# A decoder layer on one core: the last expert pair by rows with its scatter summed in PSUM, the overflow loop moved to behind pair 11, and the last normalization of both tiles interleaved

## The chip, the cores and the metric

The kernel runs on one core of a Trainium2 chip. The metric is device time in microseconds (us) of one launch. Engines are named as the profile names them: PE is the matrix engine (PEld its weight loads), DVE the vector engine, ACT the scalar engine, POOL the GpSimd engine and SP the engine whose queue issues nearly all weight transfers. A DMA is one such transfer, and it "lands" when its semaphore says that the data are there.

## What is computed

One layer for 256 tokens of width 1024: an attention and retention block, a cross attention over 256 memory tokens, and a mixture of 32 experts, each followed by a layer normalization. The change touches the experts and the last normalization alone.

```python
def moe(x, router_w, router_b, w_gate, b_gate, w_up, b_up, w_down, b_down):
    logits = xf @ router_w + router_b
    top_val, top_idx = lax.top_k(logits, 4)
    top_w = jax.nn.softmax(top_val, axis=-1)
    ...
    def step(y, blk):
        e, tok, wt = blk
        xb = xf[tok]
        gate = jnp.minimum(xb @ w_gate[e] + b_gate[e], 7.0)
        up = jnp.clip(xb @ w_up[e] + b_up[e], -7.0, 7.0)
        hmid = gate * jax.nn.sigmoid(1.702 * gate) * (up + 1.0)
        out = hmid @ w_down[e] + b_down[e]
        return y.at[tok].add(out * wt[:, None])
...
f = moe(x, ...)
x = layer_norm(DEEPNORM_ALPHA * x + f, ln3_g, ln3_b)
```

All arithmetic is float32. The three weights of an expert hold 4 MB each, so the 32 experts bring 403 MB through the DMA queues.

## The kernel before

The first part of the layer (attention, retention, cross attention, router) takes about the first 265 us and is not touched.

The experts are worked in 16 pairs, pr = 0 to 15. A pair has 64 token slots for each of its two experts, so 128 rows in all. For each pair: `masks` (L934, DVE) builds the one-hot matrix `oh` of tokens and slots; `gather` (L951 on PE, L955 on ACT) picks the tokens' columns into `xg`; `ff` (L991 bias, L983 products) multiplies by `w_gate`, then by `w_up`; `gate` (L1007 to L1009) and `swiglu` (L1015, L1016) apply the activation on DVE and ACT; `h_t` (L1025, L1026) transposes the result; `down` (L983) multiplies by `w_down` and `scaled` (L976, ACT) weighs the rows; `back` (L964, L966) transposes `oh`; and `scatter` (L1046 on PE, L1047 on DVE) adds the rows onto the two token tiles of the sum `y`. The scatter of pair pr is done inside `ff` of `w_gate` of pair pr+1, after its first quarter, and the gather of pair pr+1 stands between `w_up` and `w_down` of pair pr.

The order on each engine is written out by hand, in program order. Weights stream through SBUF in tiles of 2 MB ("doubles": half of one expert's weight): four tiles for each weight of a pair, twelve for a pair. `stream_get` takes two tiles at a time, and `pump_doubles` issues the next loads in the list whenever enough doubles are free; about ten of them are in use or in flight. All these loads wait in one queue, that of SP (L1083), and SP issues a load when the tile's former readers are done and the load eight places earlier has landed.

The last pair stands apart (L1249 onward). Its `w_up` and the first half of its `w_down` come in 512-column parts and the second half in 256-column parts, in 16 and 18 smaller loads. The products are made column by column (`cols_mm`, L1257): after each part of `down` follow `scaled`, `scatter` and the normalization's statistics (L613) for those columns. Then the hand-written order is closed and `extra` (L1177) runs: a loop over a number read at run time, for experts that got more than 64 tokens. With these inputs it runs zero times, but its branches and the meeting of all engines ahead of it remain. Behind it `Norm.finish` handles tile 0, then tile 1: L617 mean and variance, L368 and L369 (POOL) the reciprocal root, L632 centring, L638 scaling, and L1290 the four output transfers.

Of the kernel before, what the change touches and what calls it, by code (L numbers as in the profile page):

```python
# [28 lines left out]
AHEAD = 3  # L29
SLOTS = (1, 10, 18, 13, 20, 7, 19, 17, 16, 14, 5, 3, 0, 2, 21, 9, 8, 11, 6, 12, 15, 4)  # L30
# [44 lines left out]
def _body(tc, nc, ctx, I, out, dbg):  # L75
# [7 lines left out]
    manual.enter_context(tc.manual_schedule())  # L83

# [505 lines left out]
    class Norm:  # L590
# [3 lines left out]
        def __init__(self, o, g, b, z=None):  # L594
            self.o, self.g, self.b, self.z = o, g, b, z
            self.bs = sm.tile([P, 2, 4, 6], F32, name="bs", tag="bs")
            self.mv = sm.tile([P, 2, 4], F32, name="mv", tag="mv")
# [12 lines left out]
        def stats(self, t, cs):  # L610

            for q in range(cs.start // 256, cs.stop // 256):
                nc.vector.bn_stats(out=self.bs[:, t, q, :], in_=self.o[t][:, 256 * q:256 * q + 256])  # L613

        def rstd(self, t, n=2):
            mv = self.mv[:, t, :]
            nc.vector.bn_aggr(out=mv[:, 0:2], in_=self.bs[:, t, 0:n])  # L617
            rsqrt_eps(mv[:, 2:3], mv[:, 1:2], 1)
# [10 lines left out]
        def center(self, t):  # L629
            for c in range(2):  # L630
                y = self.o[t][:, half[c]]
                nc.vector.scalar_tensor_tensor(out=y, in0=y, scalar=self.mv[:, t, 0:1], in1=self.g[:, half[c]],  # L632
# [9 lines left out]

        def finish(self, t, each=None):
            self.rstd(t, 4)
            self.center(t)
            self.scale(t, each)
# [347 lines left out]
    def ff(xg, selt, j, get, mid=None):  # L994
        ps = biased(selt, j)
        for kk in range(4):
# [4 lines left out]
            if kk == 0 and mid:  # L1001
                mid()
# [39 lines left out]
    def scatter(o, ohT, cs=half, after=None):  # L1042
        for c in cs:
            for t in range(2):
                py = tr_tile()[:, 0:c.stop - c.start]
                nc.tensor.matmul(py, ohT[:, tok[t]], o[:, c], start=True, stop=True)  # L1046
                nc.vector.tensor_tensor(out=y[t][:, c], in0=y[t][:, c], in1=py, op=ALU.add)  # L1047
                if after:
                    after(t, c)
# [6 lines left out]

    for pr in range(1, NPAIR):
        for n in ("w_gate", "w_up", "w_down")[:3 if pr < NPAIR - 1 else 1]:
            for a in range(2):
                for e in range(2):  # L1060
                    loads.append(([4, D], [(0, lambda t: t, fours(I[n][0, 2 * pr + e])[:, a])]))

    def col_parts(n, c0, cn, k0, *ks):

        for a, b in zip(ks, ks[1:]):
            for e in range(2):
                yield e, lambda t, a=a, b=b: t[:, k0 + a:k0 + b, :], \
                    fours(I[n][0, NE - 2 + e])[:, a // 4, a % 4:a % 4 + b - a, c0:c0 + cn]


    for c in range(2):
        loads.append(([KC, 512], [*col_parts("w_up", 512 * c, 512, 0, 0, 4, 8)]))
    loads.append(([KC, 512], [*col_parts("w_down", 0, 512, 0, 0, 4, 6, 8)]))
    loads.append(([2 * KC, 256], [*col_parts("w_down", 512, 256, 0, 0, 4, 8),
                                  *col_parts("w_down", 768, 256, KC, 0, 4, 6, 8)]))

    def load_double():

        shape, parts = loads.pop(0)
        ts = [tile8(shape, weight=True, n=2) for _ in range(1 + max(e for e, _, _ in parts))]  # L1080
        got.extend(ts)
        for e, dst, src in parts:
# [92 lines left out]
    def extra():  # L1175

        with tc.For_i(0, n_extra, 1) as i:  # L1177
# [32 lines left out]
            scatter(down(h_t(u, as_t(ta)), getter("w_down"), ohT, tb), ohT, after=n3.stats)  # L1210
# [16 lines left out]

    prev = None
    oh = static_masks(0)
    selt = static_pick(0)  # L1230
    xg = gather(oh)
    for pr in range(NPAIR - 1):
# [4 lines left out]
        ps = ff(xg, selt, 0, stream_get, (lambda: scatter(*prev)) if pr else None)  # L1237
# [5 lines left out]
        oh = static_masks(pr + 1)  # L1243
# [84 lines left out]
```

## Time and profile before

| | us |
|---|---|
| median of 3 runs (lowest, highest) | 1182.46 (1181.59, 1185.07) |
| time of the profiled execution | 1185.23 |
| its span, first to last instruction | 1183.3 |
| PE busy | 1124.9 (95%) |
| DVE, ACT, POOL busy | 323.8, 233.9, 28.5 |
| bytes moved by DMA | 447.66 MB, 378 GB/s over the span |

The table's busy times are sums over the whole span. How far an engine is the bound differs by stretch, and the rows further down are read by stretch: a row of a timeline is a run of like instructions on one engine, with its start, its length, and in brackets the idle time ahead of it and what ended it.

### The profile page before, as it was taken

The numbers are of one execution on the slowest core, as the hardware profiler recorded it, in microseconds if no ns is written. First come the engines' busy times: TensorE is split into PE (matmuls) and PEld (weight loads), VectorE is DVE, ScalarE is ACT, GpSimd is POOL, SyncE is SP. The second block draws the span as 40 slices with busy tenths as digits, with TensorE's granted clock in tenths as the row PEclk, the third lists the DMA queues.
The fourth block names the chain that finished last, engine by engine and source line by source line (L and its number), as shares of the span: only waits on it lengthen the run. The fifth ranks groups of instructions, "written<-read, shape, count | busy, mean of one in ns | idle before, by whom it ended". The sixth has DMA issues, their size and how long they took to land. (4 is left out here: it accounts for less than half of the span.)

```text
span 1183.3 us, 12818 instructions
## 1 busy us (share of the span) xinstructions
PE 1124.9 (95%) x5473; PEld 558.4 (47%) x5473; DVE 323.8 (27%) x461; ACT 233.9 (20%) x433; POOL 28.5 (2%) x37
## 2 busy tenths in 40 slices
PE   8999999999999999999999998989899989999985
PEld 6788899864333434343343434343334343433332
DVE  5666866662121110112110101010101010102114
ACT  5543455431010101010111011010011010120100
POOL 0102300100000000000000000000000000000000
PEclk9999999999989999999999999999999999989998
DMA  9937538589999999999999999999999999999994
GB/s 333 388 125 280 183 133 320 185 349 415 417 397 417 431 425 429 427 428 428 428 428 427 429 426 428 428 427 430 425 429 427 426 430 425 430 427 428 414 372 141
DMA packets 60928, 447.66 MB, mean 378 GB/s; under 512 B 5186, under 2 KB 10050, under 8 KB 35524
## 3 DMA queue, kind: packets, MB, share of 16 engines
q1 hardware_dynamic: 60484, 446.15, 91.7%
q8 instruction: 45, 0.74, 0.3%
q10 hardware_dynamic: 384, 0.66, 0.2%
q14 instruction: 15, 0.12, 0.0%
HBM read 445.73 MB, written 1.05 MB: 378 GB/s over the span
## 5 line engine op out<-in xcount | busy, mean ns | idle before, releaser
L983 PE MATMUL mm<-t,t 128*64 128x512 f32 x2944 | 670.0, 602 | 21.6 <-DMA t<-in_w_up_dram 18.3
L983 PEld LDWEIGHTS mm<-t,t 128*64 128x64 f32 x2944 | 217.6, 138 | 445.9 <-issue 406.7
L1047 DVE TENSOR_TENSOR t<-t,tr 128x512 f32<-128x512 f32 (+1 forms) x66 | 44.2, 670 | 376.0 <-PE tr L1046 376.0
L256 PE MATMUL mm<-t,t 128*128 128x512 f32 (+1 forms) x368 | 129.4, 352 | 1.1 <-ACT t L142 1.1
L257 PE MATMUL mm<-t,t 128*128 128x512 f32 (+1 forms) x368 | 127.0, 345 | 1.0 <-DVE t L143 1.0
L258 PE MATMUL mm<-t,t 128*128 128x512 f32 (+1 forms) x368 | 126.7, 344 | 0.0
L955 ACT ACTIVATE t<-tr,gb 128x128 f32<-128x128 f32 x128 | 48.2, 456 | 259.4 <-PE tr L951 240.4
L143 DVE TENSOR_TENSOR t<-t,t 128x1024 fp32r<-128x1024 f32 (+2 forms) x74 | 86.3, 1181 | 31.2 <-ACT t L142 30.7
L1015 DVE TENSOR_SCALAR mm<-mm 128x512 f32<-128x512 f32 x32 | 22.4, 699 | 216.0 <-PE mm L983 202.7
L142 ACT CAST t<-t 128x1024 fp32r<-128x1024 f32 (+1 forms) x76 | 73.8, 999 | 37.7 <-DVE t L143 15.0
L1008 ACT ACTIVATE t<-mm 128x1024 f32<-128x1024 f32 x16 | 16.4, 1024 | 301.7 <-DVE mm L1007 301.7
L256 PEld LDWEIGHTS mm<-t,t 128*128 128x128 f32 x368 | 69.8, 190 | 12.1 <-ACT t L142 2.7
L257 PEld LDWEIGHTS mm<-t,t 128*128 128x128 f32 x368 | 69.8, 190 | 9.5 <-DVE t L143 2.1
L258 PEld LDWEIGHTS mm<-t,t 128*128 128x128 f32 x368 | 69.8, 190 | 8.3
L1046 PE MATMUL tr<-t,ohT 128*128 128x512 f32 (+1 forms) x132 | 62.6, 605 | 2.0 <-ACT t L976 1.4
L951 PEld LDWEIGHTS tr<-oh,t 128*128 128x128 f32 x512 | 58.4, 192 | 12.6 <-issue 12.2
L951 PE MATMUL tr<-oh,t 128*128 128x128 f32 x512 | 61.4, 278 | 0.0
L1007 DVE TENSOR_SCALAR mm<-mm 128x1024 f32<-128x1024 f32 x16 | 19.7, 1233 | 152.1 <-PE mm L983 152.1
L976 ACT ACTIVATE t<-mm,ohT 128x1024 f32<-128x1024 f32 (+2 forms) x18 | 18.3, 1019 | 213.6 <-PE mm L983 196.5
L1046 PEld LDWEIGHTS tr<-t,ohT 128*128 128x128 f32 x132 | 21.1, 188 | 43.4 <-issue 19.8
L1025 PE MATMUL tr<-ident,t 128*128 128x128 f32 x128 | 23.6, 307 | 17.1 <-ACT t L955 15.5
L1257 PE MATMUL mm<-t,t 128*64 128x512 f32 (+1 forms) x160 | 28.8, 511 | 1.6 <-DVE t L1016 1.6
(166 smaller groups left out, 471.8 us busy)
## 6 DMA issues: line engine op xcount, KB each, us to landing
t<-in_w_gate_dram SPq DMA_DIRECT2D x60, 2048.0 KB, 35.0
t<-in_w_up_dram SPq DMA_DIRECT2D x56, 2048.0 KB, 34.0
t<-in_w_down_dram SPq DMA_DIRECT2D x56, 2048.0 KB, 31.7
t<-in_w_up_dram SPq DMA_DIRECT2D x16, 1024.0 KB, 10.5
t<-in_w_in_dram SPq DMA_DIRECT2D x12, 1024.0 KB, 14.2
t<-in_w_down_dram SPq DMA_DIRECT2D x10, 1024.0 KB, 11.4
t<-in_w_gate_dram SPq DMA_DIRECT2D x8, 1024.0 KB, 7.0
t<-in_w_down_dram SPq DMA_DIRECT2D x10, 512.0 KB, 10.9
```

Source lines behind the costliest of these rows:

```text
L142: h(out=hi, in_=src)
L143: l(out=lo, in0=src, in1=hi.bitcast(F32))
L256: nc.tensor.matmul(ps, lh, rh, start=start, stop=False)
L257: nc.tensor.matmul(ps, lh, rl, start=False, stop=False)
L258: nc.tensor.matmul(ps, ll, rh, start=False, stop=stop)
L951: nc.tensor.matmul(px[:, c, :], zn[t][:, chunk(4 * j + c)], oh[:, t, :], start=(c == 0 and t == 0), stop=(c == 3 and t == 1))
L955: nc.scalar.activation(out=xg[:, k, :], in_=px[:, c, :], func=AF.Identity, scale=gb[:, 0, k:k + 1], bias=gb[:, 1, k:k + 1])
L983: nc.tensor.matmul(ps[r, half[c]], lhs[:, 2 * kk + k, r], w(e, k), start=(first and k == 0), stop=(last and k == 1))
L1025: nc.tensor.transpose(ph[:, c, :], u[:, cols(4 * j + c)], ident)
L1046: nc.tensor.matmul(py, ohT[:, tok[t]], o[:, c], start=True, stop=True)
L1047: nc.vector.tensor_tensor(out=y[t][:, c], in0=y[t][:, c], in1=py, op=ALU.add)
L1257: nc.tensor.matmul(ps[r, :], lhs[:, k0 + k, r], w[e][:, j0 + k, :], start=(k0 + k == 0 and lhs is not xg), stop=(k0 + k == KC - 1))
```

## The change

Three things are done.

The overflow loop `extra` moves from the end to behind pair 11 (`EXTRA = 11`). Pair 11 no longer has the gather of pair 12 between its products; it scatters its own rows at once, all engines meet at the loop, and `start_pair(12)` (masks, pick, gather) follows. While pair 11's `down` runs, `hold[0] = 3` keeps three doubles free for the loop's own tiles; the hold falls behind the loop. The load of the last normalization's two parameter rows (`load_rows`) comes behind the loop too, as its place in the program did not change.

The last pair's weights come by rows in nearly the same tiles as all other pairs', with the last four tiles of `w_up` and `w_down` cut into 1 MB and smaller loads. Its products run in the order of the other pairs. In the midst of its `w_up`, `y_sums` copies `y` into two PSUM tiles `ys` by a product with the identity, and the last scatter accumulates on them, so the four DVE additions of that scatter are gone. The swiglu, the first half of `h_t` and `down` now follow each other without overlap between column halves of `w_up`.

The last normalization reads `ys` in PSUM: statistics and centring of tile 0, statistics of tile 1, scaling of tile 0, centring and scaling of tile 1, with statistics over 512 columns at a time.

```diff
+EXTRA = 11
...
     def pump_doubles():
-        while loads and doubles() >= 1 + max(e for e, _, _ in loads[0][1]):
+        while loads and doubles() >= 1 + hold[0] + max(e for e, _, _ in loads[0]):
             load_double()
...
         ohT = static_back(oh, pr)
-        oh = static_masks(pr + 1)
+        if pr != EXTRA:
+            oh = static_masks(pr + 1)
         u = swiglu(ff(xg, selt, 1, stream_get, add_bias if pr == 1 else None), g)
-        xg, selt = gather(oh), static_pick(pr + 1)
+        if pr != EXTRA:
+            xg, selt = gather(oh), static_pick(pr + 1)
+        hold[0] = 3 if pr == EXTRA else 0
         prev = (down(h_t(u), stream_get, ohT, mid=spread_rows if pr == NPAIR - 3 else None), ohT)
...
+        if pr == EXTRA:
+            scatter(*prev)
+            prev = None
+            n_extra = nc.values_load(ni32[0:1, 0:1], min_val=0, max_val=3 * NPAIR)
+            manual.close()
+            extra()
+            manual.enter_context(tc.manual_schedule())
+            hold[0] = 0
+            oh, selt, xg = start_pair(pr + 1)
...
+    def y_sums():
+        ys.extend(mm_tile() for _ in range(2))
+        for t in range(2):
+            for c in half:
+                nc.tensor.matmul(ys[t][:, c], ident, y[t][:, c], start=True, stop=False)
+
+    u = swiglu(ff(xg, selt, 1, stream_get, {1: y_sums}), g)
+    hT = h_t(u, cs=(0,))
...
+                if kk == 3 and k == 1:
+                    scaled(o[:, half[c]], ps[:, half[c]], ohT)
+        done()
+        if kk == 0:
+            h_t(u, hT, (1,))
...
+    for t in range(2):
+        for c in range(2):
+            nc.tensor.matmul(ys[t][:, half[c]], ohT[:, tok[t]], o[:, half[c]], start=False, stop=True)
+            n3.stats(t, c)
+        n3.rstd(t)
+        if t == 0:
+            n3.center(0)
...
+    n3.scale(0, store)
+    n3.center(1)
+    n3.scale(1, store)
     manual.close()
-    extra()
-    for t in range(2):
-        n3.finish(t, each=lambda t, c: (nc.sync, nc.scalar)[c].dma_start(out=o_v[:, t, half[c]],
```

In the rows that follow, L1077 is the weight load (L1083 before), L1171 the loop, L1253 the reading of its count, L978 the products of a pair, L1042 the scatter, L946 the gather.

SP's queue around pair 12's `w_up`, before (tiles t_564 to t_569 are pair 12's `w_gate`, t_572 to t_577 its `w_up`, t_581 its `w_down`):

```order
L1083 DMA t_569_4574<-in_w_gate_dram 128x4096 [waits DMAHW3_49,PE_49]
L1083 DMA t_572_4639<-in_w_up_dram 128x4096 [waits DMAHW4_49,PE_49]
L1083 DMA t_573_4641<-in_w_up_dram 128x4096 [waits DMAHW5_49,PE_49]
L1083 DMA t_576_4659<-in_w_up_dram 128x4096 [waits DMAHW6_49,PE_49]
L1083 DMA t_577_4661<-in_w_up_dram 128x4096 [waits DMAHW7_49,PE_49]
L1217 DMA t_580_4681<-in_ln_g_dram 1x1024 [waits DMAHW0_49]
L1217 DMA t_580_4681<-in_ln_b_dram 1x1024 [waits DMAHW1_49]
L1083 DMA t_581_4687<-in_w_down_dram 128x4096 [waits DMAHW2_49,PE_49]
```

The same place of SP's queue in the changed kernel, up to the loop:

```order
L1077 DMA t_569_4572<-in_w_gate_dram 128x4096 [waits DMAHW3_49,PE_49]
L1077 DMA t_574_4624<-in_w_up_dram 128x4096 [waits DMAHW4_49,PE_49]
L1253 TENSOR_LOAD ni_2180 [waits DVE_49]
L1171 COMPARE_AND_BRANCH
L1171 UNCONDITIONAL_BRANCH [waits DMAHW0_49,DMAHW1_49,DMAHW2_49,DMAHW3_49,DMAHW4_49,DMAHW5_49,DMAHW6_49,DMAHW7_49]
```

And behind the loop:

```order
L1253 ISA x2
L1212 DMA t_583_4926<-in_ln_g_dram 1x1024
L1212 DMA t_583_4926<-in_ln_b_dram 1x1024
L1077 DMA t_584_4932<-in_w_up_dram 128x4096
L1077 DMA t_585_4934<-in_w_up_dram 128x4096
L1077 DMA t_586_4936<-in_w_up_dram 128x4096
L1077 DMA t_587_4938<-in_w_down_dram 128x4096
L1077 DMA t_588_4940<-in_w_down_dram 128x4096
L1077 DMA t_591_4958<-in_w_down_dram 128x4096 [waits PE_49]
```

One load of pair 12's `w_up` now stands ahead of the loop and three behind it, and at the branch SP waits for the semaphores of all eight DMA slots.

PE behind pair 11's `down` (t_560 and t_561 are the last two tiles of its `w_down`), in the changed kernel, up to the loop:

```order
L978 MATMUL mm<-t_561_4515,t_4594 64x512
L1042 MATMUL tr<-t_4642,ohT 128x512 [waits Activation_49]
L1042 MATMUL tr<-t_4642,ohT 128x512 [waits PE_49]
L1042 MATMUL tr<-t_4642,ohT 128x512 [waits DVE_49] x2
L1253 TENSOR_LOAD ni_2180 [waits DVE_49]
L1171 COMPARE_AND_BRANCH
L1171 UNCONDITIONAL_BRANCH [waits PE_49]
L1171 UNCONDITIONAL_BRANCH [waits barrier_Pool_Activation_PE_DVE_SP_release]
```

And behind it (t_564 and t_565 are pair 12's first `w_gate` tiles):

```order
L946 MATMUL tr<-oh,t_262_1997 128x128 [waits DVE_49]
L946 MATMUL tr<-oh,t_262_1997 128x128 x15
L986 MATMUL mm<-t_1996,selt 128x512 [waits DVE_49]
L986 MATMUL mm<-t_1996,selt 128x512
L978 MATMUL mm<-t_564_4550,t_4899 64x512 [waits Activation_49]
```

Before, the bias and the products of pair 12's `w_gate` stood straight behind that `down`; now the scatter, the meeting of the engines and the gather stand between them.

PE at the end of the changed kernel (t_5668 is `hT`, t_663 and t_664 the last tiles of `w_down`, t_5676 is `o`):

```order
L1281 MATMUL mm<-t_663_5583,t_5668 64x512 [waits DMAHW2_49,Activation_49]
L1281 MATMUL mm<-t_664_5584,t_5668 64x512 [waits DMAHW3_49]
L1292 MATMUL mm<-t_5676,ohT 128x512
L1292 MATMUL mm<-t_5676,ohT 128x512 [waits DVE_49,Activation_49]
L1292 MATMUL mm<-t_5676,ohT 128x512
L1292 MATMUL mm<-t_5676,ohT 128x512 [waits DVE_49]
```

All four scatter products now stand behind the whole of `down`, where two of them stood between its column parts.

## Rows read from the trace of the kernel before

**Rows 1.** Page, span in 40 equal slices: what the DMA queues moved.

```profile
GB/s 333 388 125 280 183 133 320 185 349 415 417 397 417 431 425 429 427 428 428 428 428 427 429 426 428 428 427 430 425 429 427 426 430 425 430 427 428 414 372 141
```

**Rows 2.** DMA view: issues, count, KB each, median us from issue to landing.

```profile
t<-in_w_gate_dram SPq DMA_DIRECT2D x60, 2048.0 KB, 35.0
...
out_dram<-t SPq DMA_DIRECT2D x2, 256.0 KB, 2.1
```

**Rows 3.** Timeline of SP's queue: start, length, operation; pair 12's w_up loads.

```profile
911.16 14.77 SPq L1083 DMA_DIRECT2D t<-in_w_up_dram  x4
```

**Rows 4.** Timeline of PE, pairs 11 to 14: start, length, operation, idle before.

```profile
904.89 7.08 PE L983 MATMUL mm<-t,t 128*64 128x512 f32 x30 [2.20 <-DMA t<-in_w_up_dram]
911.90 3.84 PE L951 MATMUL tr<-oh,t 128*128 128x128 f32 x32
...
918.02 13.95 PE L983 MATMUL mm<-t,t 128*64 128x512 f32 x64
931.90 0.73 PE L991 MATMUL mm<-t,selt 64*128 64x512 f32 x2
...
937.85 3.89 PE L1046 MATMUL tr<-t,ohT 128*128 128x512 f32 x8
...
963.63 7.08 PE L983 MATMUL mm<-t,t 128*64 128x512 f32 x30 [2.20 <-DMA t<-in_w_up_dram]
...
990.64 0.73 PE L991 MATMUL mm<-t,selt 64*128 64x512 f32 x2
...
1022.73 8.78 PE L983 MATMUL mm<-t,t 128*64 128x512 f32 x30 [2.56 <-DMA t<-in_w_up_dram]
...
1044.57 4.43 PE L1225 MATMUL tr<-t,ones_f 1*128 1x512 f32 x8
1048.93 9.78 PE L983 MATMUL mm<-t,t 128*64 128x512 f32 x32
1058.64 0.73 PE L991 MATMUL mm<-t,selt 64*128 64x512 f32 x2
```

**Rows 5.** Stretches: us, busy of PE to POOL (count), granted clock, DMA share, GB/s.

```profile
1020.00:1030.00 10.00, 7.44 (x28) 2.33 (x28) 0.00 (x0) 0.00 (x0) 0.00 (x0) 0.83 1.02 434
...
1130.00:1140.00 10.00, 9.38 (x46) 3.31 (x42) 3.00 (x3) 1.48 (x4) 0.00 (x0) 1.00 1.05 386
```

**Rows 6.** Timeline of PE, pair 14's down and the last pair.

```profile
1098.53 13.95 PE L983 MATMUL mm<-t,t 128*64 128x512 f32 x64
...
1112.41 0.73 PE L991 MATMUL mm<-t,selt 64*128 64x512 f32 x2
...
1132.29 7.09 PE L1257 MATMUL mm<-t,t 128*64 128x512 f32 x32
...
1159.05 1.98 PE L1046 MATMUL tr<-t,ohT 128*128 128x512 f32 x4 [0.85 <-ACT t L976]
...
1166.28 3.67 PE L1257 MATMUL mm<-t,t 128*64 128x256 f32 x32
```

**Rows 7.** Timeline of DVE, pair 14's mask and swiglu, and the end.

```profile
1080.82 0.42 DVE L934 TENSOR_TENSOR oh<-posm,iota 128x256 f32<-128x256 f32 x1
1092.55 0.70 DVE L1015 TENSOR_SCALAR mm<-mm 128x512 f32<-128x512 f32 x1 [11.31 <-PE mm L983]
...
1094.75 0.69 DVE L1016 SCALAR_TENSOR_TENSOR t<-mm,t 128x512 f32<-128x512 f32 x1
...
1160.94 0.75 DVE L613 BATCH_NORM_STATS2 bs<-t 128x6 f32<-128x256 f32 x2
...
1174.23 0.26 DVE L617 BATCH_NORM_AGGREGATE mv<-bs 128x2 f32<-128x24 f32 x1 [1.30 <-issue]
...
1174.85 1.41 DVE L632 SCALAR_TENSOR_TENSOR t<-t,mv,t 128x512 f32<-128x512 f32 x2
...
1178.88 1.41 DVE L638 SCALAR_TENSOR_TENSOR t<-t,mv,t 128x512 f32<-128x512 f32 x2
```

**Rows 8.** The loop's line on PE: count, ns min/median/max, first and last start.

```profile
L1177 PEldq COMPARE_BRANCH  x3: 97/196/3782, 1170.6 to 1176.6; - x3
```

More of the change, by code (lines that the diff above doesn't have):

```diff
@@ L608, in take, with stats, rstd @@
             nc.vector.bn_stats(out=self.bs[:, t, c, :], in_=y)
[L610 to L615, printed above, removed]
+        def stats(self, t, c):
+            nc.vector.bn_stats(out=self.bs[:, t, c, :], in_=self.src[t][:, half[c]])
+        def rstd(self, t):
             mv = self.mv[:, t, :]
-            nc.vector.bn_aggr(out=mv[:, 0:2], in_=self.bs[:, t, 0:n])
+            nc.vector.bn_aggr(out=mv[:, 0:2], in_=self.bs[:, t, 0:2])
             rsqrt_eps(mv[:, 2:3], mv[:, 1:2], 1)
@@ L1000, in ff @@
             done()
-            if kk == 0 and mid:
-                mid()
+            if kk in mids:
+                mids[kk]()
         return ps
@@ L1040, in down, with scatter @@
         return o
-    def scatter(o, ohT, cs=half, after=None):
-        for c in cs:
+    def scatter(o, ohT):
+        for c in half:
             for t in range(2):
-                py = tr_tile()[:, 0:c.stop - c.start]
+                py = tr_tile()
                 nc.tensor.matmul(py, ohT[:, tok[t]], o[:, c], start=True, stop=True)
                 nc.vector.tensor_tensor(out=y[t][:, c], in0=y[t][:, c], in1=py, op=ALU.add)
-                if after:
-                    after(t, c)
     wpos = [NPRE]
@@ L1209, in extra @@
             u = swiglu(ff(xg, selt, 1, getter("w_up")), g)
-            scatter(down(h_t(u, as_t(ta)), getter("w_down"), ohT, tb), ohT, after=n3.stats)
+            scatter(down(h_t(u, as_t(ta)), getter("w_down"), ohT, tb), ohT)
+            free8(tab, *ws2)
     LN3 = {}
@@ L1226, in spread_rows, with start_pair @@
                 nc.scalar.copy(out=gb3[:, j, half[c]], in_=pt)
+    def start_pair(pr):
+        oh = static_masks(pr)
+        selt = static_pick(pr)
+        return oh, selt, gather(oh)
     prev = None
-    oh = static_masks(0)
-    selt = static_pick(0)
-    xg = gather(oh)
+    oh, selt, xg = start_pair(0)
     for pr in range(NPAIR - 1):
@@ L1236, in _body @@
             load_rows()
-        ps = ff(xg, selt, 0, stream_get, (lambda: scatter(*prev)) if pr else None)
+        ps = ff(xg, selt, 0, stream_get, (lambda: scatter(*prev)) if prev else None)
         if pr == 0:
@@ L1248, in _body @@
             tables()
-    n_extra = nc.values_load(ni32[0:1, 0:1], min_val=0, max_val=3 * NPAIR)
-    g = gate(ff(xg, selt, 0, stream_get, lambda: scatter(*prev)))
-    def cols_mm(ps, lhs, w, k0, j0):
-        for k in range(4):
-            for e in range(2):
-                r = slice(64 * e, 64 * e + 64)
-                nc.tensor.matmul(ps[r, :], lhs[:, k0 + k, r], w[e][:, j0 + k, :],
-                                 start=(k0 + k == 0 and lhs is not xg), stop=(k0 + k == KC - 1))
-    ohT = static_back(oh, NPAIR - 1)
@@ new lines, in _body @@
+    n3 = Norm(y, LN3["gb"][:, 0, :], LN3["gb"][:, 1, :], src=ys)
+    o_v = out.rearrange("(t p) d -> p t d", p=P)
+    for t in range(2):
+        for c in range(2):
+            nc.tensor.matmul(ys[t][:, half[c]], ohT[:, tok[t]], o[:, half[c]], start=False, stop=True)
[3 more added lines that the diff above has]
+            n3.center(0)
+    store = lambda t, c: (nc.sync, nc.scalar)[c].dma_start(out=o_v[:, t, half[c]], in_=y[t][:, half[c]])
+    n3.scale(0, store)
+    n3.center(1)
```

82 lines of the change are left out of this document (33 added, 49 removed).

## The prediction

> **What bounds the kernel now.** I read the stretches first, then PE's timeline, then SP's queue. Through the expert pairs the DMA queues move 425 to 430 GB/s without a break until the last slices [rows 1]. A weight tile of 2048 KB [rows 2] is 2.097 MB, so at 428 GB/s it takes 4.90 us, and twelve tiles, a pair, 58.8. PE's timeline bears it out: its waits for the fourth `w_up` tile of pair 11 and of pair 12 end at 904.89 and 963.63 [rows 4], 58.74 apart, which is 4.895 a tile. Where PE has no transfer to wait for it needs less for a pair: from pair 14's bias at 1058.64 [rows 4] to pair 15's at 1112.41 [rows 6] are 53.77 us, and no row of that stretch ends a wait for a DMA. So the stream is the bound until PE's last wait for it, which ends at 1022.73 [rows 4]; from there on PE is, because the work at 1044.57 and a low clock put it behind. What counts for the end is therefore when PE can run without waits, and how much work it then has.
>
> **The loop behind pair 11.** The meeting of the engines needs SP, and SP's branch waits for the semaphores of all eight DMA slots (the order of SP's queue). So PE cannot go on before everything in flight has landed. In flight at that point are the loads up to the first `w_up` tile of pair 12; that load's turn comes at 911.16 as before [rows 3], since nothing changes ahead of it. Behind the tile landed at 904.89 come four of pair 11's `w_down`, four of pair 12's `w_gate` and this one: 9 x 4.895 = 44.05, so the last lands at 948.94.
>
> PE itself is there long before. Its `down` of pair 11 must wait for its fourth tile (904.89 + 4 x 4.895 = 924.5), then half of 13.95 [rows 4] gives 931.5, the scaling about 1, the scatter 3.89 [rows 4]: 937. It idles 12 us. What I save in pair 11 (no gather between `w_up` and `down`) is swallowed by this wait and counts nothing.
>
> Restart. The branches and semaphores of the loop take DVE 1.30 from its last operation to its next at the end of the kernel before [rows 7]; then the mask 0.42 [rows 7], then the gather can start: 948.94 + 1.72 = 950.66. PE's own branch took up to 3.78 [rows 8]; it comes before the meeting and PE has 12 us for it, so I count 0 and keep 3.8 as the upper end. The gather takes 3.84 [rows 4], now with nothing beside it.
>
> The clock. After a wait of 2.56 us the granted clock of a stretch was 0.83 [rows 5], that is, some of it at 1.2 GHz in place of 2.4, and the half phase behind it took 8.78 where the one at 904.89 took 7.08: 1.7 lost. After the thin row products at 1044.57 a half took 9.78 in place of 7.09 [rows 4, 6]: 2.69 lost. Nothing shows 12 idle us; bounds are 0 and 3.8 (the whole gather at half rate), and I take 2.7, the costlier of the two rows, as the idle time is longer than either. A rule of the Trainium skill speaks against the change here: "TensorE: Matmul & The Clock Gate", Part 1: The HAM clock gate, says that the throttled clock is the default and that sustained activity releases it, so that work behind an idle engine begins at half rate. The two rows agree; by the rule the zero end falls away and the sum stays.
>
> So pair 12's `w_gate` phase starts at 950.66 + 3.84 + 2.7 = 957.2, against 931.90 before [rows 4]: 25.3 later.
>
> From there PE saves. First the scatter of pair 11, already done: 3.9. Second all waits: before, from 931.90 to 1112.41 three pairs took 180.51. Pair 12 took 58.74 (931.90 to 990.64), 4.97 over 53.77. Pair 13 took 68.00 (to 1058.64), 14.23 over; of that 4.36 is the parameter rows' spreading (1044.57 to 1048.93) and 2.69 the clock behind it, both of which stay, so 7.18 is waiting and its clock. Together 12.15. In the changed kernel PE is late enough that the tiles are there: at 957.2 all of pair 12's `w_gate` and one tile of `w_up` lie in SBUF. SP issues the next at about 948.94 + 1.3 + some 1.2 for its two small row loads; a transfer's landing costs some 2.1 beside its bytes (256 KB, [rows 2]), so the first lands near 958.5 and each next 4.9 later, three `w_up` tiles by 968.3, where PE wants the last near 980. That margin of 9 us and more holds in the later pairs, as PE takes 53.8 a pair plus the spreading's 7 and the stream 58.8.
>
> PE thus leaves pair 14 at 957.2 - 3.9 + 180.5 - 12.15 = 1121.7, against 1112.41: **9.3 us later**. The loads still to go are 43 tiles, the last landing near 958.5 + 42 x 4.9 = 1164; PE wants it at about 1173 (below).
>
> **The last pair.** Before, 1112.41 to the end of the last column part, 1166.28 + 3.67 = 1169.95 [rows 6]: 57.54. After, in order: bias, `w_gate` with scatter, `back` and bias 19.88 (1112.41 to 1132.29, [rows 6], unchanged); `w_up` 13.9 [rows 6]; the four identity products on `y`: two scatter products took 1.98 with their pipeline's end [rows 6], so 3.6 (3.4 to 4.0); swiglu with nothing beside it 2.9 (1092.55 to 1095.44, [rows 7]) and hand-overs, 3.2, in which the first transposes and their copy lie too; `down` 13.9 and the second transposes in it 0.6 (four of the gather's instructions at 3.84 / 32, and the hand-over). Sum 55.1, so **2.4 us less**. The rows in place of columns also bring the last 16 MB at 428 GB/s instead of 386 [rows 5], some 4 us of the stream, but PE waits for nothing there, so it counts nothing.
>
> The end. Before: 1169.95 to 1183.3, 13.35. After `down`: scaling of the second half overlaps the first product; four products of 0.9 in a row end at 3.5; statistics of tile 0 (0.75 for 512 columns, [rows 7]) end at 2.7, aggregation 0.4, then DVE is full: centring 1.4, statistics of tile 1 1.5, aggregation 0.4, scaling, centring, scaling 3 x 1.35 [rows 7], which ends at 10.4; from DVE's last row (1178.88 + 1.41 = 1180.29) to the span's end were 3.0. Sum 13.4, so **0**. What the loop cost there (1.3) and the four additions save is paid back by four scatter products in one row and by DVE's seven long operations behind them. Reading the sums from PSUM costs DVE nothing that shows: L1015 reads PSUM at 0.70 and L632 SBUF at half of 1.41 [rows 7].
>
> **Sum.** +9.3 - 2.4 + 0 = +6.9. The profiled execution took 1185.23, so 1192.1 by its own time. The median is 2.77 below it. Of that, 1.7 can be the low clock behind the wait at 1022.73, which the changed kernel does not have anyway, so I take off between 1.1 and 2.8: 1189.3 to 1191.0. I say **1190.0**.
>
> **Rivals.** *The meeting does not wait for the transfers.* Then the engines pass near 938, PE goes on and meets the stream as before, SP's five held loads go out at 939 against 914 to 944 before, so the stream never stops, and only the last pair's 2.4 are left: 1182.46 - 2.4 = 1180, within 0.3% of before (0.3%, 3.5 us, is about what a measurement of this kernel can tell from no change). For it: the loop runs zero times. Against it: SP's branch names all eight slots. It decides whether PE idles 1 or 13 us at the loop. 0.09.
>
> *PE's branch comes late.* If the code behind the jump is fetched only after the meeting, 3.78 is added [rows 8], and a longer stay at the low clock adds up to 1.1: 1194 to 1195. Against it: PE arrives 12 us early. 0.15.
>
> *The loss is smaller.* No time at the low clock (-2.7) and a little less in the last pair (statistics earlier, -1): 1186.3, at the edge of "slower". 0.10.
>
> *The stream becomes the bound again*, if its restart takes over 9 us more than I have it: each us beyond is a us at the end, 1191 and up. The rows show no such restart; 0.04.
>
> **How the numbers follow.** My forecast (1188 to 1192.5) has 0.62, the rivals 0.09, 0.15, 0.10 and 0.04. The range 1186 to 1194.5 takes in the clock's two ends, the identity products' 0.6 and the offset to the median, most of the late branch, and leaves out the first rival. Faster by over 0.3% (under 1178.9) would need the first rival with some us more from the last pair: 0.03. Within 0.3% (to 1186.0): the rest of the first rival and half of the third, 0.12. Slower: 0.85.
>
> **What would show it.** Right: PE idle some 13 us behind pair 11's scatter, near 937 to 951; GB/s down in one slice there and no wait of PE for a DMA behind it; pair 14's end near 1122; `down` of the last pair ending near 1177; DVE full from there to the last store. Wrong: an idle time near 1 us at the loop, or waits for `w_up` and `w_gate` tiles in pairs 13 and 14, which would mean that the stream and not PE sets the end.

## The result and the profile after

| | before | after |
|---|---|---|
| median (lowest, highest), 6 runs each | 1183.08 (1181.59, 1185.33) | 1194.97 (1190.11, 1196.92) |
| profiled execution, its span | 1185.23, 1183.3 | 1196.92, 1194.8 |
| mean granted clock of that execution | 0.986 | 0.976 |

The change costs 11.9 us: the ratio of after to before is 1.009, with an interval of 1.0063 to 1.0116. The forecast was 1190.0 and the range's top 1194.5, so direction and mechanism came as forecast, and the median lies 0.5 us above the range. The range was set on the first median of before, 1182.46; on that one the ratio of 1.009 makes 1193.1, inside it. The six runs of the changed kernel lie 6.8 us apart, more than those of before, and go with the mean granted clock: 0.987 and 0.988 in the runs of 1190.11 and 1190.17, 0.976 to 0.982 in the four from 1194.7 to 1196.92. The profiled execution is the slowest of the six.

The page's slices (each 29.9 us) show where the stream of weights stops. Slice 32 moves 322 GB/s, where the slices of before around it have 425 to 430 [rows 1], and its granted clock falls to 0.7.

```profile
PEclk9999999999989999999999999999999799999998
...
GB/s 333 385 108 282 183 138 315 194 350 417 416 398 416 427 428 427 427 430 427 427 428 428 428 427 427 428 428 427 428 427 429 322 429 429 428 426 428 426 417 50
```

PE's timeline around the loop (start, length, operation, idle before and what ended it; L978 products of a pair, L1042 scatter, L946 gather, L986 bias), against [rows 4]:

```profile
906.18 7.08 PE L978 MATMUL mm<-t,t 128*64 128x512 f32 x30 [2.16 <-DMA t<-in_w_up_dram]
...
934.10 3.89 PE L1042 MATMUL tr<-t,ohT 128*128 128x512 f32 x8 [1.26 <-ACTq L1171]
951.34 6.53 PE L946 MATMUL tr<-oh,t 128*128 128x128 f32 x32 [13.36 <-DVE oh L929]
957.81 0.73 PE L986 MATMUL mm<-t,selt 64*128 64x512 f32 x2
```

PE has finished pair 11 at 937.99 and waits 13.36 us. The row names the mask on DVE, but DVE itself was held by SP until the loop let go:

```profile
950.86 0.42 DVE L929 TENSOR_TENSOR oh<-posm,iota 128x256 f32<-128x256 f32 x1 [12.15 <-SPq L1171]
```

SP issued nothing between the first `w_up` load of pair 12 and 951.89:

```profile
912.45 0.33 SPq L1077 DMA_DIRECT2D t<-in_w_up_dram  x1
951.89 0.30 SPq L1212 DMA_DIRECT2D t<-in_ln_g_dram  x1
952.24 0.22 SPq L1212 DMA_DIRECT2D t<-in_ln_b_dram  x1
952.51 1.30 SPq L1077 DMA_DIRECT2D t<-in_w_up_dram  x3
```

What it waited for is in its rows on the loop's line. From 913.4 on it had five waits, which ended at 930.6, 935.5, 940.4, 945.3 and 950.1: 4.9 us apart, the time of one tile. Nine tiles behind the one that landed at 906.18 make 906.18 + 44.05 = 950.2, the end of the fifth (who waited for whom, us in total, times, longest):

```profile
SPq L1171 <- SPq L1171: 36.7, 5, 17.2
```

The DMA view of 940 to 962 us (40 slices of 0.55 us) shows the queues running dry and starting again. They move full rate until about 944, then 330 falling to 180 while the last two tiles land (SP's waits that end at 945.3 and 950.1), next to nothing from 948.8 to 953.2, and full rate again from about 955:

```profile
GB/s 387 417 357 477 357 477 447 387 328 298 238 179 209 209 179 179 30 0 0 0 15 0 0 15 417 60 209 328 387 447 477 477 447 477 387 447 387 387 387 447
```

The stretches tell what the gather paid (us, then busy time of PE, PEld, DVE, ACT, POOL with counts, granted clock, DMA share, GB/s):

```profile
940.00:950.00 10.00, 0.00 (x0) 0.00 (x0) 0.00 (x0) 0.00 (x0) 0.00 (x0) 0.67 0.67 283
950.00:960.00 10.00, 8.66 (x42) 7.26 (x44) 0.56 (x2) 3.00 (x8) 0.00 (x0) 0.65 0.68 261
```

After 906.18 no row of PE ends a wait for a DMA. Pair 15's bias starts at 1120.70, against 1112.41 [rows 6]. PE's timeline of pair 13's spreading (L1220) and of the end (L1269 the products on `y`, L1281 `down`, L1292 the last scatter):

```profile
1054.51 3.77 PE L1220 MATMUL tr<-t,ones_f 1*128 1x512 f32 x8
1058.22 8.79 PE L978 MATMUL mm<-t,t 128*64 128x512 f32 x32
...
1120.70 0.73 PE L986 MATMUL mm<-t,selt 64*128 64x512 f32 x2
...
1147.60 3.70 PE L1269 MATMUL mm<-t,ident 128*128 128x512 f32 x8
1151.23 7.09 PE L978 MATMUL mm<-t,t 128*64 128x512 f32 x32
1159.94 0.72 PE L1021 MATMUL tr<-ident,t 128*128 128x128 f32 x4 [1.62 <-DVE t L1012]
1161.35 5.35 PE L1281 MATMUL mm<-t,t 128*64 128x512 f32 x16 [0.69 <-ACT t L1022]
1166.63 0.75 PE L1021 MATMUL tr<-ident,t 128*128 128x128 f32 x4
1167.31 9.66 PE L1281 MATMUL mm<-t,t 128*64 128x512 f32 x44
1177.85 1.08 PE L1281 MATMUL mm<-t,t 128*64 128x512 f32 x4 [0.87 <-ACT t L971]
1178.86 1.13 PE L1292 MATMUL mm<-t,ohT 128*128 128x512 f32 x2
1180.87 1.95 PE L1292 MATMUL mm<-t,ohT 128*128 128x512 f32 x4 [0.88 <-DVE bs L613]
1185.11 1.51 PE L1292 MATMUL mm<-t,ohT 128*128 128x512 f32 x2 [2.29 <-DVE bs L613]
```

And rows of ACT and DVE at the end (L971 `scaled`, L631 centring, L613 statistics, L638 scaling):

```profile
1177.11 0.69 ACT L971 ACTIVATE t<-mm,ohT 128x512 f32<-128x512 f32 x1 [9.10 <-PE mm L1281]
1180.02 0.70 DVE L613 BATCH_NORM_STATS2 bs<-mm 128x6 f32<-128x512 f32 x1 [18.77 <-PE mm L1292]
...
1183.05 1.40 DVE L631 SCALAR_TENSOR_TENSOR t<-mm,mv,t 128x512 f32<-128x512 f32 x2
1184.36 0.69 DVE L613 BATCH_NORM_STATS2 bs<-mm 128x6 f32<-128x512 f32 x1
1186.65 0.70 DVE L613 BATCH_NORM_STATS2 bs<-mm 128x6 f32<-128x512 f32 x1 [1.60 <-PE mm L1292]
...
1190.36 1.41 DVE L638 SCALAR_TENSOR_TENSOR t<-t,mv,t 128x512 f32<-128x512 f32 x2
```

PE waits three times in the last 18 us, each time for the reader of the *other half* of the PSUM tile it is about to write. The last products of `down`, on the second half of its tile, wait 0.87 until ACT has scaled the first half. The scatter product on the second half of `ys[0]` waits 0.88 for the statistics of the first, and that of `ys[1]` waits 2.29, because on DVE its statistics stand behind the centring of tile 0 (1183.05, two of 0.7). From 1120.70 to the span's end are 74.1 us; before, from 1112.41, 70.9.

### The profile page after: what moved, and what is told of

Same layout as the page of the kernel before. It is cut to its first block, busy times and chain, and to the rows that moved or that the text cites. A ratio compares the mean times of both kernels' runs of the same rounds, so it can differ in the third digit from the quotient of the medians.

```text
span 1194.8 us, 12742 instructions
## 1 busy us (share of the span) xinstructions
PE 1129.5 (95%) x5445; PEld 559.6 (47%) x5445; DVE 320.3 (27%) x451; ACT 233.7 (20%) x432; POOL 28.2 (2%) x37
## 3 DMA queue, kind: packets, MB, share of 16 engines
HBM read 445.73 MB, written 1.05 MB: 374 GB/s over the span
## 5 line engine op out<-in xcount | busy, mean ns | idle before, releaser
L978 PE MATMUL mm<-t,t 128*64 128x512 f32 x3008 | 679.8, 603 | 14.1 <-DMA t<-in_w_up_dram 13.4
L978 PEld LDWEIGHTS mm<-t,t 128*64 128x64 f32 x3008 | 220.7, 139 | 444.2 <-issue 418.5
L1043 DVE TENSOR_TENSOR t<-t,tr 128x512 f32<-128x512 f32 x60 | 41.2, 687 | 347.8 <-PE tr L1042 347.8
L946 PE MATMUL tr<-oh,t 128*128 128x128 f32 x512 | 64.1, 286 | 13.4 <-DVE oh L929 13.4
L946 PEld LDWEIGHTS tr<-oh,t 128*128 128x128 f32 x512 | 61.1, 199 | 26.0 <-DVE oh L929 14.2
L1042 PE MATMUL tr<-t,ohT 128*128 128x512 f32 x120 | 58.3, 618 | 1.3 <-ACTq L1171 1.3
L971 ACT ACTIVATE t<-mm,ohT 128x1024 f32<-128x1024 f32 (+1 forms) x17 | 18.1, 1063 | 207.4 <-PE mm L978 197.0
L1021 PE MATMUL tr<-ident,t 128*128 128x128 f32 x128 | 23.9, 310 | 18.5 <-ACT t L950 14.5
L1042 PEld LDWEIGHTS tr<-t,ohT 128*128 128x128 f32 x120 | 19.1, 188 | 40.3 <-DVE t L1043 19.7
L1021 PEld LDWEIGHTS tr<-ident,t 128*128 128x128 f32 x128 | 18.1, 210 | 23.8 <-ACT t L950 17.1
```

Source lines behind the costliest of these rows:

```text
L946: nc.tensor.matmul(px[:, c, :], zn[t][:, chunk(4 * j + c)], oh[:, t, :], start=(c == 0 and t == 0), stop=(c == 3 and t == 1))
L978: nc.tensor.matmul(ps[r, half[c]], lhs[:, 2 * kk + k, r], w(e, k), start=(first and k == 0), stop=(last and k == 1))
L1021: nc.tensor.transpose(ph[:, c, :], u[:, cols(4 * j + c)], ident)
```

## The experiments

Theory A is the prediction's: the meeting of the engines waits for everything in flight, and the price is the idle time and the low clock behind it. The part that the result added to A: at the end PE waits on halves of one PSUM tile. The kernels ran in three groups, and each group timed before anew: 1184.30 for the first four (13 runs), 1184.37 for the next four (13), 1183.71 for the last three (27). Kernels of different groups are compared by their ratio to before, in which the changed kernel has 1.009.

### The loop alone

The kernel before, with its own last pair, got the change's part on the loop and nothing else.

```diff
+        hold[0] = 3 if pr == EXTRA else 0
...
+        if pr == EXTRA:
+            scatter(*prev)
...
+            extra()
...
-    extra()
```

> The kernel before with the overflow loop alone moved to behind pair 11 (with the hold of three tiles and pair 12's start behind it); the last pair by columns and the old normalization stay, without a loop at the end. Theory A (the meeting of the engines waits for five weight tiles in flight, PE idles some 13 us and hands on 8.3 us of it): PE idle 13 to 14 us ahead of pair 12's gather, pair 14 ends near 1120.7 instead of 1112.4, and with the 1.3 us of the loop at the end gone the time is some 7 us over before, near 1190. Rival B (the new last pair and normalization cost most of the change): at most 3 us over before.

Measured: 1191.52 (4 runs), ratio 1.0071 [1.0051, 1.0092], 7.2 us over before. In its PE timeline PE idles as long as in the changed kernel, and pair 15 begins at 1119.68, 7.3 after before's 1112.41:

```profile
950.75 6.10 PE L953 MATMUL tr<-oh,t 128*128 128x128 f32 x32 [13.39 <-DVE oh L936]
...
1119.68 0.73 PE L993 MATMUL mm<-t,selt 64*128 64x512 f32 x2
```

Its end, with the old last pair and no loop, is 69.3 us long (1119.68 to 1189.0), 1.6 under before's 70.9, so the 7.2 already have that saving in them. The move of the loop alone makes most of the loss. The rival in which the meeting passes without the transfers is out.

### Everything but the loop

The changed kernel with the loop and its hold left out altogether. It leaves out the handling of experts with more than 64 tokens, which these inputs never need.

```diff
-EXTRA = 11
+EXTRA = 99
```

> The changed kernel without the overflow loop and its hold (the handling of experts with more than 64 tokens is left out; with these inputs it runs zero times). Theory A: pair 14 ends as before near 1112.4, and only the new last pair remains, 74.1 us in the changed kernel against 70.9 before, or 72.4 where its down phase runs at the full clock: 1.5 to 3.2 us over before, some 8 to 9 us under the changed kernel. Rival B: still 7 us or more over before.

Measured: 1186.09 (10 runs), ratio 1.0016 [1.0005, 1.0027]. So the other two parts of the change, which the prediction had at 2.4 us less, cost 1.8 more, although this kernel also saves the meeting at the end. Its tail, from pair 15's bias at 1111.60 to the span's end at 1185.9, is 74.3, and its PE timeline has the same three waits:

```profile
1168.41 1.08 PE L1281 MATMUL mm<-t,t 128*64 128x512 f32 x4 [0.87 <-ACT t L971]
1169.42 1.12 PE L1292 MATMUL mm<-t,ohT 128*128 128x512 f32 x2
1171.43 1.96 PE L1292 MATMUL mm<-t,ohT 128*128 128x512 f32 x4 [0.88 <-DVE bs L613]
1175.70 2.08 PE L1292 MATMUL mm<-t,ohT 128*128 128x512 f32 x2 [2.32 <-DVE bs L613]
```

The expectation had 72.4 for a tail whose `down` runs at the full clock. It did run so (15.9 us, in place of 17.6 in the changed kernel), but the tail is no shorter, because other rows are longer: the first sixteen products of pair 15 took 4.66 in place of 3.65, a half of `w_up` 7.44 in place of 7.09, the last scatter products 2.08 in place of 1.51. Why they are longer is not shown.

7.2 and 1.8 make 9.0, but both kernels are without the loop at the end, so its 1.3 us [rows 7] are taken off twice. With them counted once, the two parts make 10.3 of the 11.9; the remaining 1.6 lie inside the interval of the whole (7.5 to 13.7 us), and no run settles them.

### The tail without its waits

The two halves of the last `down` go to two PSUM tiles, and the scatter goes column half by column half, so that two products on one tile no longer follow each other; the normalization's first steps stand behind all four.

```diff
-    ps = mm_tile()
+    pc = [mm_tile()[:, 0:512], None]
...
+        if kk == 0:
+            pc[1] = tr_tile()
...
-    for t in range(2):
-        for c in range(2):
+    for c in range(2):
+        for t in range(2):
...
-        n3.rstd(t)
-        if t == 0:
-            n3.center(0)
+    n3.rstd(0)
+    n3.center(0)
+    n3.rstd(1)
```

> The changed kernel with its end alone altered: the two column halves of the last down product lie in two separate PSUM tiles, and the last four scatter products go through both token tiles of a half before the next half, with the statistics in the same order and tile 0's centring behind them. Theory D (three waits on a tile whose other half is still being read, 0.87, 0.88 and 2.29 us, cost the end what they last): these waits vanish from PE's rows, and from the start of the last down product to the end it is 3 to 4 us shorter; the time is 3 to 4 us under the changed kernel. Rival E (DVE is full behind the first statistics anyway): 1 us or less.

Measured: 1191.62 (4 runs), ratio 1.0068 [1.0049, 1.0087], 3.35 us under the changed kernel's median and 2.6 under it by the ratios, whose intervals overlap. The trace is clearer than the times. The eight instructions of the last scatter are one run, DVE waits for nothing but PE, and the tail is 70.6 (1118.55 to 1189.2) in place of 74.1. From the start of `down` to the end are 30.0 us in place of 33.5, with the low clock at the start of `down` in both. Three rows of its PE timeline:

```profile
1159.21 1.97 PE L1283 MATMUL mm<-t,t 128*64 128x512 f32 x4 [0.69 <-ACT t L1022]
1160.95 1.80 PE L1283 MATMUL tr<-t,t 128*64 128x512 f32 x4
...
1175.62 3.96 PE L1294 MATMUL mm<-t,ohT 128*128 128x512 f32 x8
```

What is left is in the first two of these rows: runs of four products that take 1.03 further on in the same `down` took 1.97 and 1.80 there. In the best form below the same place took 1.08 and 1.05, and the tail was 69.3.

### A deeper hold, so that less is in flight

With one double more kept free, PE should meet the loop with one tile fewer outstanding.

```diff
-        hold[0] = 3 if pr == EXTRA else 0
+        hold[0] = 4 if pr == EXTRA else 0
```

> The changed kernel with one number altered, a hold of four tiles in place of three, so that the first up tile of pair 12 is issued behind the loop and four tiles instead of five are in flight at the meeting. Theory A (PE waits there for what is in flight): PE idle shrinks by one tile's 4.9 us, from 13.4 to 8.5; the stream restarts 4.9 us earlier too and loses no more than before, so pair 14 ends 3 to 4.9 us earlier than 1120.7, and the time is 3 to 5 us under the changed kernel. Rival C (the idle time is branches and the fetching of code behind the jump): idle 13 us and the time as they are.

Measured: 1194.2 (4 runs), ratio 1.0075 [1.0051, 1.0099]: no gain that the times show. The mechanism did what A says: SP has four waits at the loop instead of five, the last ending at 946.7, the idle time fell by 4.77, one tile of the stream, and pair 12 began 3.8 earlier, at 954.04. But 2.9 of the 3.8 were spent in pair 13, so that pair 15 began at 1119.87, only 0.8 earlier. Of these, 1.3 went at the `w_up` of pair 13, where PE met the stream again, and 1.65 into the parameter rows (3.77 in the changed kernel, 4.21 here) and the half behind them (8.79, and 10.00 here). That the stream loses no more than before did not hold either: the page's slice of the loop has 290 GB/s instead of 322, (427 - 290) / 427 x 29.8 = 9.6 us lost instead of 7.4. Its PE timeline:

```profile
947.96 6.15 PE L946 MATMUL tr<-oh,t 128*128 128x128 f32 x32 [8.59 <-DVE oh L929]
954.04 0.73 PE L986 MATMUL mm<-t,selt 64*128 64x512 f32 x2
...
1031.89 7.08 PE L978 MATMUL mm<-t,t 128*64 128x512 f32 x30 [0.22 <-DMA t<-in_w_up_dram]
...
1052.03 4.21 PE L1220 MATMUL tr<-t,ones_f 1*128 1x512 f32 x8
1056.17 10.00 PE L978 MATMUL mm<-t,t 128*64 128x512 f32 x32
```

The link from what is in flight to PE's idle time is shown; that it is worth time by itself is not.

### The spreading of the parameter rows in an earlier pair

The eight thin products that spread the normalization's rows, with the low clock behind them, go from pair 13 to pair 9, where PE waits for the stream anyway.

```diff
-        if pr == NPAIR - 4:
+        if pr == 8:
...
-        prev = (down(h_t(u), stream_get, ohT, mid=spread_rows if pr == NPAIR - 3 else None), ohT)
+        prev = (down(h_t(u), stream_get, ohT, mid=spread_rows if pr == 9 else None), ohT)
```

> The changed kernel with the loading and the spreading of the last normalization's parameter rows moved from pairs 12 and 13 to pairs 8 and 9, where PE waits for the weight stream. Theory A (behind the loop PE is the bound to the end): the 3.8 us of row products and the 1.7 us of low clock behind them in pair 13 are saved in full; pair 14 ends near 1115 and the time is 5 to 7 us under the changed kernel. Rival G (the weight stream, with its gap at the loop, is the bound behind it): at most 1 us.

Measured: 1190.83 (10 runs), ratio 1.0047 [1.0029, 1.0065], 4.1 under the changed kernel's median and 5.1 by the ratios, whose intervals just touch. The spreading took 4.68 and the half behind it 9.52 in pair 9, and neither shows behind it: PE's wait for the stream in pair 11 still ends at 904.49, after 2.20 of waiting. Pair 15's bias moved from 1120.70 to 1113.54, 7.2 earlier. Of these, 1.7 were there ahead of the loop (904.49 against 906.18) and 5.5 are the spreading and the clock behind it in pair 13; and now PE reaches the stream once more. Its PE timeline there:

```profile
1113.54 0.73 PE L986 MATMUL mm<-t,selt 64*128 64x512 f32 x2
1114.20 1.07 PE L978 MATMUL mm<-t,t 128*64 128x512 f32 x2
1115.90 3.65 PE L978 MATMUL mm<-t,t 128*64 128x512 f32 x14 [0.63 <-DMA t<-in_w_gate_dram]
```

So behind the loop PE is the bound, as the prediction had it, but with only some 5 us before the stream is the bound again.

### The loop at other places

Three kernels move the loop forward: behind pair 7 with nothing else changed, and behind pair 1 and pair 0, both with the tail without its waits and the early spreading.

```diff
-EXTRA = 11
+EXTRA = 7
```

> The changed kernel with the overflow loop behind pair 7 in place of 11. Theory A (PE's idle time at the meeting is paid at the end only where too few waits for the weight stream follow to use it up; what always remains is the gap in the stream, 960.23 - 950.12 - 4.9 = 5.2 us): PE is some 25 us late at pair 8, its waits in pairs 8 to 12 vanish, from pair 12 or 13 on it waits for the stream again, and pair 14 ends near 1117.6 where the changed kernel has 1120.7 and the kernel before 1112.4: 3 us under the changed kernel. Rival F (the idle time costs the same wherever it lies): as the changed kernel.

Measured: 1196.0 (4 runs), ratio 1.0097 [1.0064, 1.0131]. Its profiled execution is by far the quickest of the four (1191.78; the others 1195.95 to 1197.56), and it alone goes A's way, with an idle time of 14.68 and pair 15 at 1115.2. The times show no gain, which is rival F's number; between the two it is not settled.

```diff
-EXTRA = 11
+EXTRA = 1
```

> The end of a_tail and the early spreading of a_spread9, with the overflow loop behind pair 1. Theory A: PE's idle time at the loop is used up by the waits of pairs 5 to 13, the gap in the stream costs 0 to 5 us, as the stream is not yet at its full rate there (398 to 417 GB/s), and with the last pair at 68.5 to 70.6 us the span is 1178 to 1184, as before or up to 5 us faster. Rival F: 1190 or more.

```diff
-EXTRA = 11
+EXTRA = 0
```

> As a_best1 with the overflow loop behind pair 0, where only some three weight tiles are in flight when PE gets there (12 us from issue to landing) and the stream is still short of its full rate. Theory A: the gap in the stream costs 0 to 3 us; span 1178 to 1182, a little under a_best1. Rival F: 1190 or more.

Measured: 1198.17 (ratio 1.0109 [1.0076, 1.0142]) and 1196.51 (1.0093 [1.0059, 1.0126]), 4 runs each. Both expectations were missed by over 10 us; rival F's number came, but not by its reason. Behind pair 0 PE's own idle time is only 5.20, and yet the stream loses more than behind pair 11. The stretch from 300 to 320 us, in this kernel and then in before (columns as in the stretches above):

```profile
300.00:320.00 20.00, 13.50 (x54) 6.54 (x51) 3.31 (x6) 1.11 (x1) 0.00 (x0) 0.85 0.47 173
```

```profile
300.00:320.00 20.00, 20.00 (x84) 6.43 (x82) 2.75 (x4) 1.11 (x1) 0.00 (x0) 1.00 1.01 414
```

(414 - 173) x 20 / 428 = 11.3 us of the stream are gone. The DMA view of 296 to 322 us in the kernel with the loop behind pair 0 (40 slices of 0.65 us) shows that most of them are lost ahead of the meeting:

```profile
GB/s 76 25 0 0 0 0 0 0 0 0 0 0 0 0 0 0 0 277 126 353 429 479 454 479 429 202 38 0 0 13 25 328 126 328 403 429 429 429 454 403
```

The queues stand still from 297.3 to 307, while PE works on `down` until 306.1. SP issues one load at 283.39, one at 306.10, when it had waited 14.7 us for PE's products, and the next behind the loop at 315.27. So here SP waits for PE, and the stream stands still ahead of the meeting; behind pair 11 it runs up to the meeting, and PE waits for it. What ends last behind pair 0 is PE's own branch at the loop, 3.78 long (311.5 to 315.3); SP's wait for the one tile ended at 314.0. Behind pair 1 it is much the same: no load between 345.83 and 370.05, the queues nearly at rest from 355.5, PE at work until 368.6. How much of this is the hold and how much the order of SP's queue was not tried.

PE's wait for pair 13's `w_up` in the kernel with the loop behind pair 0 ends at 1038.99, against 1022.73 [rows 4]:

```profile
1038.99 7.08 PE L978 MATMUL mm<-t,t 128*64 128x512 f32 x30 [2.70 <-DMA t<-in_w_up_dram]
```

Behind pair 11 the lost stream, (427 - 322) / 427 x 29.9 = 7.4 us by the slices, is hidden behind PE's lateness. Early it is the loss itself, as the stream is the bound until pair 13. Of the 16.3 us between the two waits, the 20 us ahead of the stretch above hold another 4.3 (336 GB/s against 428), and the 60 us behind it win 2.3 back (423, 424 and 428 against 395, 413 and 417). That makes some 13; the rest is open.

### The best form with the loop behind pair 11

Tail without waits, early spreading, hold of 4.

> The changed kernel, loop behind pair 11, with the end of a_tail, the early spreading of a_spread9 and the hold of four of a_hold4. Theory A: pair 12's gate phase starts near 953 and PE meets the weight stream again in pairs 13 and 14, so pair 14 ends near 1113 to 1116; the last pair takes 68.5 to 70.6 us; span 1182 to 1187, time 1184 to 1189, 6 to 10 us under the changed kernel and 0 to 5 over before. Rival (the three gains overlap wholly): no less than a_spread9's 1190.8.

Measured: 1187.8 (10 runs), ratio 1.0035 [1.0017, 1.0052], the changed kernel's interval lying wholly above. It is 6.5 us under the changed kernel by the ratios and still slower than before. Pair 15's bias starts at 1114.56, the span ends at 1183.9, and 69.3 us lie between, as many as in the kernel with the loop alone, which has the old last pair. So without its waits the new last pair is as long as the old one without the loop, and no gain of its own shows. PE waits for the stream twice again in pair 14 (0.64 and 2.19).

### Before, with the two good parts

The kernel before with the early spreading alone, and the kernel before with the last pair by rows, two PSUM tiles in `down`, its scatter added on `y` in SBUF as before, the interleaved normalization, the early spreading, and the loop where it was.

```diff
+        if pr == 8:
...
+        prev = (down(h_t(u), stream_get, ohT, mid=spread_rows if pr == 9 else None), ohT)
```

> The kernel before with the loading and the spreading of the last normalization's parameter rows moved from pairs 12 and 13 to pairs 8 and 9. Theory A (before, PE falls behind the weight stream only by that work of 4.4 us and the low clock behind it, 2.7 us): PE waits for the stream up to the last pair, whose loads by columns then set the end; 1 to 4 us under before. Rival H (those 7 us are hidden or come back elsewhere): no change.

```diff
+    u = swiglu(ff(xg, selt, 1, stream_get), g)
...
+    pc = [mm_tile()[:, 0:512], None]
...
+    scatter(o, ohT, after=n3.stats)
     manual.close()
     extra()
...
+    n3.scale(0, store)
+    n3.center(1)
+    n3.scale(1, store)
```

> As b_spread, with the last pair's weights and products by rows as in the changed kernel and two PSUM tiles for the halves of its down product, but with its scatter added onto y in SBUF by DVE, the overflow loop at the end, and the interleaved normalization behind it. Theory A: the stream ends some 4 us earlier, the end from the last down product on is some 4 us longer than before (four additions and statistics on DVE in a row, then the loop's 1.3); 0 to 4 us under before. Rival: the end's extra length outweighs it, up to 3 us over before.

Measured: 1185.02 (11 runs), ratio 1.0004 [0.999, 1.0017], and 1183.64 (11 runs), 1.0002 [0.9989, 1.0016]. Neither differs from before: the 1 to 4 us of the first expectation were not measured, its rival's "no change" was, and the second cannot be told from 0. In the trace of the first, the spreading leaves pair 13 and pair 15's bias comes at 1107.3, 5.1 earlier, but PE now waits for the stream in pairs 14 and 15, and the medians show nothing of it. Its PE timeline:

```profile
1080.24 7.08 PE L983 MATMUL mm<-t,t 128*64 128x512 f32 x30 [2.28 <-DMA t<-in_w_up_dram]
...
1109.60 3.65 PE L983 MATMUL mm<-t,t 128*64 128x512 f32 x14 [0.61 <-DMA t<-in_w_gate_dram]
```

No version here is measurably faster than before.

## Why the prediction was right, and where it was short

**The bound.** Right. PE's last wait for the stream is the one that ends at 906.18, and from the loop on PE sets the end. The early spreading shows it: what it saves in pair 13 is saved at pair 15. The margin ahead of the stream was smaller than the "9 us and more" that the forecast gave the later pairs. With 5.5 us saved PE waits for a weight tile in pair 15 (0.63), and in the deeper hold it does so in pair 13 (0.22). By the forecast's own figures a pair takes PE 53.8 and the stream 58.8, so the 9 us shrink by 5 in pair 12 alone.

**The meeting waits for all transfers.** Right in place and size: pair 11 done at 937.99 (forecast 937), idle 13.36 (12 to 13), gather from 951.34 (950.66), SP's first weight load 952.51 (about 951.4). The last tile landed at 950.1 where 948.94 was written, because PE's wait for the stream in this execution ends 1.3 later than before's, at 906.18; from there on the nine tiles took what was forecast. The hold kernel shows the cause: a tile fewer in flight, 4.77 less idle.

**The clock.** The gather took 6.53 where it took 3.84 [rows 4], 2.69 lost; 2.7 was taken, from a row of another kind of work. In the other kernels with the loop behind pair 11 the same gather took 5.98 to 6.58, so the size is right and the fit to the hundredth is chance. The granted clock was 0.67 in the idle stretch and 0.65 in the one with the gather, a mix of 2.4 and 1.2 GHz. The Trainium skill, "TensorE: Matmul & The Clock Gate", Part 1: The HAM clock gate, has work behind an idle engine begin at half rate, and the trace agrees here. Pair 12's `w_gate` began at 957.81 (957.2).

**Pair 14's end.** 1120.70 where 1121.7 was forecast; +8.3 instead of +9.3. The difference is in pair 13, where the spreading took 3.77 and the half behind it 8.79, 1.65 less than the rows of before that the forecast kept, against a start 0.6 later. The loop alone put pair 15 off by 7.3 in its trace, so this term was a little too large.

**The last pair and the end.** This is the step that failed. It was -2.4 and 0; the tail grew by 3.2 in the trace (74.1 against 70.9), and the kernel without the loop measured +1.8. The parts up to `down` fit: `w_gate` with its bias 19.88 (19.88), `w_up` and the products on `y` 17.7 (17.5), the hand-over 3.0 (3.2). `down` took 17.6 where 14.5 was written: 0.87 of waiting for ACT, 1.7 at the low clock behind the hand-over (5.35 for sixteen instructions that take 3.65 in the kernel without the loop), and 0.5 that stays open. Behind it came 15.9 instead of 13.4: "scaling of the second half overlaps the first product; four products of 0.9 in a row end at 3.5" is wrong, as the products ended at 1185.11 + 1.51 = 1186.6, 7.7 behind `down`'s end, with 0.88 and 2.29 of waiting in them. The program order of the changed kernel, shown above ahead of the prediction, has these waits word for word (`L1292 ... [waits DVE_49,Activation_49]`, `[waits DVE_49]`, `L1281 ... [waits DMAHW2_49,Activation_49]`); I priced the products and not their waits. With the waits removed and the full clock, in the best form, the tail is 69.3, against the 68.5 that the prediction's own terms make from pair 15's bias on. So the size of the end came from waits on half tiles that the forecast had at nothing, and from a low clock in `down` that differs between executions.

**Sum and offset.** +6.9 was forecast. +8.3 and +3.2 make 11.5, which is the difference of the two spans (1194.8 - 1183.3). The median is 1.95 below the profiled execution's time, inside the 1.1 to 2.8 taken off.

**Rivals.** *The meeting does not wait* is out (13.36 idle, and the loop alone at +7.2). *PE's branch comes late* gave 1194 to 1195, and 1194.97 was measured, yet it is wrong: the loop's line on PE shows a branch of 6.06 us, longer than the 3.78 of [rows 8], that began at 938.2 and so was over at 944.3, while SP's last wait for a tile ended at 950.1. A rival's number can be met by another cause. The row is the loop's line on PE's weight-load queue from 936 to 945 us (count, ns min/median/max, first and last start):

```profile
L1171 PEldq COMPARE_BRANCH  x2: 101/3081/6061, 937.5 to 938.2; - x2
```

*The loss is smaller* is out: the gather lost 2.69 and the end grew. *The stream becomes the bound again* did not happen in the changed kernel, but does in those with less PE work behind the loop or a deeper hold.

## What to carry to other kernels

A run-time loop that runs zero times is still a meeting of all engines, and its price depends on which engine waits there for which. At the end of this kernel, with nothing in flight, it cost 1.3 us on DVE, and no other place that was tried was cheaper. Behind pair 11, in a full weight stream, PE waits for what is in flight: 13.4 us of idle time, 2.7 at the low clock, and about 7 us of the stream. Behind pairs 0 and 1 the stream stands still ahead of the meeting, while PE is still at work, and as the stream is the bound there, that loss is not hidden. When an order moves work onto PSUM, count waits by whole tiles: in this program a product on one half of a tile waits for the reader of the other half (0.87, 0.88 and 2.29 us), and the program order lists that wait before anything is run.

## What the runs showed of the hardware that was not expected

- The queues behind pair 11 did not stop at once: the rate fell to about 200 GB/s over the last 4 us and needed some 3 us behind the first new weight load to be full again (the row of 940 to 962 us). The slice loses 7.4 us of stream, not only the gap between issue and landing.
- The longest of PE's branches at the loop took 6.06 us in the changed kernel, 4.92 in the deeper hold, and 3.78 before and behind pair 0. Behind pair 11 it is over (944.3) ahead of SP's last wait (950.1); behind pair 0 it ends last (315.3 against 314.0).
- The same short hand-over (1.62 and 0.69 us of waiting ahead of `down`) was followed by the low clock in the changed kernel (5.35 for sixteen instructions), in the deeper hold and in the early spreading (5.35 each) and in the tail without waits, but not in the kernel without the loop (3.65) nor in the best form. Such differences make 1 to 2 us at a place. The six runs of the changed kernel lie 6.8 us apart, the two quickest at the higher mean clock, and effects of 2 to 4 us (the hold, the loop behind pair 7) sink in that. What decides whether the clock falls behind such a hand-over is not shown.
